# Reordering the side queue of a fused layer: the third pair's projection goes ahead of the second query's rest, the last pair's runs step by step beside the third query

## The chip, the core and the metric

The kernel is one launch on one NeuronCore of a Trainium2 chip. The metric is device time in microseconds (us). Its engines are named as in the profile: PE (matrix multiply; PEld its weight loads), DVE (vector), ACT (scalar, activations), POOL (GpSimd) and SP, which here only issues DMAs. Each engine runs its own list of instructions in order and waits on semaphores for the others.

## The reference, cut to what matters

One layer over 1024 tokens of width 1024, in two sub-layers. The part that matters here:

```python
p = adaln(x, shift1, scale1) @ w_in
y_rw = rwkv7_scan(...)            # state recurrence, in chunks of 64 tokens
y1 = concatenate([y_conv, y_rw]) @ w_out
x  = layer_norm(ALPHA * x + gate1 * y1, ln1_g, ln1_b)
h2 = adaln(x, shift2, scale2)
q  = (h2 @ peer_wq)               # 8 heads x 256
s1, s2 = q-halves against peer_k1, peer_k2   # 128 scores each
v1,i1 = top_k(s1,16); v2,i2 = top_k(s2,16)
sc,ci = top_k(v1[:,None]+v2[None,:], 16)     # 16 of 16384 experts per head
gates = softmax(sc)
y2 = sum_k gelu(h2 . peer_u[e_k]) * gates_k * peer_v[e_k]
out = layer_norm(ALPHA * x + gate2 * y2, ln2_g, ln2_b)
```

## The kernel before, in words

Tokens are cut in eight tiles of 128, and tiles in four pairs of 256. The program has two parts.

**The dense part** comes last and takes over half of the time. For tiles 0 to 4 it multiplies with all 16384 experts, `h2 @ peer_u.T` (line L1285), times a dense matrix of gates, and then `@ peer_v` (L1319). Tiles 5 to 7 are done beside it by gathering their chosen rows (L1203, L1211, L1218). The dense part needs the gate matrices of tiles 0 to 4 in memory (`gmat<-G_d`, L1260).

**The part before it** has these pieces; the short names are used in the prediction.

- The *scan*: the recurrence, 16 chunks (`for c in range(16)`, `solve` and `pass_state`, L615 to L734; L719 writes the state `SN`). It is a chain: chunk after chunk.
- `front(t0)`, F0 to F3, one per pair: loads the scan's and the convolution's output, multiplies it with `w_out` (L822, 96 matmuls of 512 columns with tiles `ychi`, `yclo`, `wsplit`, accumulated in `mm`), adds the residual (L826), normalises twice (L205 to L223, L840, L841) and stores `x1` and, for gathered tiles, `h2`.
- `query(t0)`, Q0 to Q3, one per pair: transposes the normalised rows (L231), multiplies with `wq` (`proj`, L197, 384 matmuls of 256 columns), multiplies with the keys (L894), and, for tiles 0 to 5, finds the best 16 of each 128 scores on DVE (`best16`, L782 to L786 on tiles `vi`, `s12`). Tiles 6 and 7 only store their scores.
- `choose(t)`, C0 to C5: the best 16 of the pairwise sums and their expert numbers, DVE mostly (L930 to L1002). They are put in a queue `slow`.
- `gate_matrix(t)`, G0 to G4: 32 steps a tile. Each step makes a one-hot matrix of four tokens on DVE (`mask`, L1046, one pair per two steps; L1054), POOL (L1053) and ACT (`oa`, L1052), multiplies on PE (L1057, into `mgate`) and copies the result on ACT into `stage` (L1058). Every eight steps a `stage` of 2 MB is written to `G_d` by a DMA from ACT's queue (L1065). There are two `stage` buffers and a third that only every third block of tiles 0 to 3 may use. They are put in a queue `gates`.

F and Q are generators that yield after each matmul or so (F yields twice a matmul). They stand in a list `side`; `step(side)` runs the first of it by one step. During the scan, `fill()` calls `step(side)` between the scan's own matmuls. The list gets F0, Q0 after chunk 3, F1, Q1 after chunk 7 and F2 after chunk 11. Before chunk 9 what is left of the first two (`firsts[:2 + CD]`, CD is 0) is run to its end. After the scan the rest is added and run:

```python
side += [front(S - PB, page2[0]), query(S - 2 * PB), query(S - PB)]   # F3, Q2, Q3
while side or slow or gates:
    step(side)
    fills[0] += 1
    if fills[0] % TSLOW == 0 or not side:     # TSLOW = 2
        slow_step(1)
    if fills[0] % TGATE == 0 or not side:     # TGATE = 12
        with tc.high_priority(offset=GPRI) if GPRI else nullcontext():
            step(gates)
```

So a gate step comes once in twelve steps of `side`, or in every turn when `side` is empty. This order is not the last word: a scheduler takes it as the priorities from which it makes each engine's list, and the waits follow from the data. F0 to F2 take their buffers from a pool of 30 pages (`pgp`), F3 and the choosing of tiles 4 and 5 from a second pool of 12 (`pg2`), which exists after the scan.

Of the kernel before, what the change touches and what calls it, by code (L numbers as in the profile page):

```python
# [21 lines left out]
S = 1024  # L22
# [18 lines left out]
PB = 256  # L41
# [5 lines left out]
GBUF = 6  # L47
AHEAD = 4
NMM = 3

PSG, PSD = 3, 3
SLOW = 4
# [10 lines left out]
CD = 0  # L63
# [23 lines left out]
def layer_kernel(ctx, tc, x, cols, c_row, cond_w, w_in, w2a2, g2, w_out, ln_rows, wq, keys, peer_u, peer_ut, peer_v, peer_vt, out):  # L87
# [47 lines left out]
    fex = ctx.enter_context(ExitStack())  # L135
    psum = fex.enter_context(tc.tile_pool(name="psum", bufs=NMM, space=PSUM))
    ws = fex.enter_context(tc.tile_pool(name="ws", bufs=2))
# [20 lines left out]
    def mm(w=512):  # L158
        return psum.tile([128, 512], F32, tag="mm", name="mm")[:, :w]
# [4 lines left out]
    def page(name, dt=F32, w=512):  # L164
        return pgp.tile([128, max(w, 512)], dt, tag="pg", name=name)[:, :w]
# [6 lines left out]
    def load_split(src, j, scale=None):  # L172

        both = ws.tile([128, 2, KD, 128], F32R, name="wsplit", bufs=WSPLIT)
        hi, lo = both[:, 0], both[:, 1]
        key = src.tensor.name, j
        if key in split_d:
            fetched[key] = ld(both.bitcast(F32), split_d[key])
        else:
            raw = load_raw(src[j])  # L180
            if scale is not None:
                r_ = raw.rearrange("p (k a) b -> p k (a b)", k=2)
                V.tensor_mul(r_, r_, scale[:, None, :].to_broadcast([128, 2, 512]))
            A.activation(hi, raw, AF.Copy)  # L184
            G.tensor_sub(lo, raw, hi.bitcast(F32))  # L185
            split_d[key] = dram.tile([128, 2, KD, 128], F32, name=f"split_{key[0]}{j}")
            ld(split_d[key], both.bitcast(F32))
        return hi, lo

    def proj(w, act, pt):  # L190

        whi, wlo = w
        ahi, alo = act
        i = 0
        for k in range(KD):
            for l, r in ((whi, ahi), (whi, alo), (wlo, ahi)):
                T.matmul(pt, l[:, k, :], r[k], start=i == 0, stop=i == 3 * KD - 1)  # L197
                i += 1
                yield
# [25 lines left out]
    def to_channels(xn, shift, scale, hi, lo, keep=None, ks=range(KD), bank=None):  # L225

        n = 128 * len(xn)
        for k in ks:
            pt = (bank or mm)()[:, :n]
            for i, parts in enumerate(xn):  # L230
                T.transpose(pt[:, 128 * i:128 * i + 128], parts[k // 4][:, 128 * (k % 4):128 * (k % 4) + 128], ident)  # L231
            hf = page("hf", w=n)
            A.activation(hf, pt, AF.Identity, bias=shift(k), scale=scale(k))
            A.activation(hi[k], hf, AF.Copy)
            V.tensor_sub(lo[k], hf, hi[k].bitcast(F32))
            if keep:
                keep(k, hi[k], lo[k])

    def step(jobs):
        while jobs:  # L240
            try:
                next(jobs[0])
                return
            except StopIteration:
                jobs.pop(0)

    def run(jobs):
        for j in jobs:
            yield from j
# [271 lines left out]
    def slow_step(n):  # L521
        for _ in range(n):
            while slow:
                try:
                    next(slow[0])
                    break
                except StopIteration:
                    slow.pop(0)
# [10 lines left out]

    bank = [psr.tile([128, 512], F32, name=f"bank{i}", bufs=1) for i in range(7 - NMM)]  # L540
    turn = [0, 0, 0]
# [6 lines left out]
    def mE(s):  # L548
        return bank[3 + s % (4 - NMM)].rearrange("p (a b) -> p a b", a=4)

# [37 lines left out]
    side, rate, credit, fills = [], [0.0], [0.0], [0]  # L588
# [21 lines left out]
    kept, ys, late, normed, page2, st3, blocks = {}, {}, [], {}, [], [], [0]  # L610
# [164 lines left out]
    def duo(name, dt=F32, pg_=page):  # L775

        ps = [pg_(name, dt).rearrange("p (a t) -> p a t", a=2) for _ in range(KD // 2)]
        return ps, [ps[k // 2][:, k % 2, :] for k in range(KD)]

    def best16(vs, ix, sm):  # L780

        V.max(vs[:, 0:8], sm)  # L782
        V.max_index(ix[:, 0:8], vs[:, 0:8], sm)
        V.match_replace(sm, vs[:, 0:8], sm, -3.0e38)
        V.max(vs[:, 8:16], sm)
        V.max_index(ix[:, 8:16], vs[:, 8:16], sm)  # L786
# [72 lines left out]
    def query(t0):  # L859

        n, nt, tile0 = PB, PB // 128, t0 // 128
        fetch = [tile0 + t in GT for t in range(nt)]
        xn = normed.pop(t0)
        hi, lo = duo("h2hi", F32R)[1], duo("h2lo", F32R)[1]

        def keep(k, h, l):
            for w, f in enumerate((h, l)):
                for t in range(nt):
                    if not fetch[t]:
                        d = 128 * DT.index(tile0 + t)  # L870
                        ld(h2t_d[w, k, :, d:d + 128], f[:, 128 * t:128 * t + 128].bitcast(F32))

        to_channels(xn, lambda k: mod[:, 24 + k:25 + k], lambda k: modp[:, k, 1:2], hi, lo, keep)
        yield
        vi = [page("vi").rearrange("p (q h a r) -> p q h a r", q=2, h=NH, a=2) for t in range(nt)
              if tile0 + t not in score_d]
        val = [t[:, 0] for t in vi]
        idx = [t[:, 1].bitcast(U32) for t in vi]
        for g in range(4):
            kt = pgp.tile([128, 4, 128], F32, tag="pg", name="keys")  # L880
            ld(kt, keys[:, 4 * g:4 * g + 4, :])
            qt = []
            for m in range(4):
                w = load_split(wq, 4 * g + m)
                pt = mm(n)
                yield from proj(w, (hi, lo), pt)
                if m % 2 == 0:
                    qp = page("qt").rearrange("p (a t) -> p a t", a=2)
                A.activation(qp[:, m % 2, :], pt, AF.Copy)
                qt.append(qp[:, m % 2, :])  # L890
            for t in range(nt):
                ps = mm()
                for m in range(4):
                    T.matmul(ps[:, 128 * m:128 * m + 128], qt[m][:, 128 * t:128 * t + 128], kt[:, m, :],  # L894
                             start=True, stop=True)
                s = page("s12")
                A.activation(s, ps, AF.Copy)
                if tile0 + t in score_d:
                    ld(score_d[tile0 + t][g], s)
                    yield  # L900
                    continue
                for m in range(4):
                    best16(val[t][:, 2 * g + m // 2, m % 2], idx[t][:, 2 * g + m // 2, m % 2], s[:, 128 * m:128 * m + 128])
                    yield
        for t in range(len(vi)):
            slow.append(choose(tile0 + t, val[t], idx[t], 0, NH, 4, lambda nm, d, w, p=page2[0] if t0 == S - 2 * PB and P2C else page: p(nm, d, w), V if t0 >= LV else G))
# [166 lines left out]
    flight, firsts = [[solve(1)]], []  # L1073
    for c in range(16):
        if c == 5:
            while side and side[0] is first:
                step(side)
        if c == 9:
            while conv_left and slow:
                slow_step(1)  # L1080
            while side and side[0] in firsts[:2 + CD]:
                step(side)
            fet.close()
            gb.append(fex.enter_context(tc.tile_pool(name="gb", bufs=1)))
        if c < 14:
            flight.append([solve(c + 2)])
        for _ in pass_state(c):
            for i, f in enumerate(flight):
                for _ in range(STEPS[i]):
                    step(f)  # L1090
            step(late)
        if flight:
            f = flight.pop(0)
            while f:
                step(f)
        if c % 4 == 3 and c < 15:
            while late:
                step(late)
            side.append(front(64 * (c - 3), page))
            firsts.append(side[-1])  # L1100
            if c == 3 and CD:
                side.append(run(held))
                firsts.append(side[-1])
            if c < 11:
                side.append(query(64 * (c - 3)))
                firsts.append(side[-1])
            rate[0] = RATES[1]
# [11 lines left out]
    pg2 = pg2x.enter_context(tc.tile_pool(name="pg2", bufs=NP2, side="right"))  # L1119
    page2.append(lambda name, dt=F32, w=512: pg2.tile([128, max(w, 512)], dt, tag="pg2", name=name)[:, :w])  # L1120

    side += [front(S - PB, page2[0]), query(S - 2 * PB), query(S - PB)]
    while side or slow or gates:
        step(side)
        fills[0] += 1
# [263 lines left out]
```

## Time and profile before

| | us |
|---|---|
| median of 3 runs | 3229.51 (3221.18 to 3232.97) |
| the profiled execution | 3222.35, span 3220.4 |
| PE busy in the span | 2995.8 (93%) |
| DVE busy | 2536.9 (79%) |
| POOL busy | 1759.9 (55%) |
| ACT busy | 1168.8 (36%) |
| chain that ended last | PE 41%, DVE 10%, DMA 3% |

The page gives busy time by engine, the span in 40 slices, the chain of work that ended last, and groups of instructions by line. A busy PE is not PE at its peak: matmuls overlap, and the clock that was granted (PEclk) is told beside it. `L12` is line 12 of the kernel before; an order of the kernel after has lines one higher in this part of the program (L823 is L822), and nine higher behind the change.

### The profile page before, as it was taken

Reading aid. Unit: us, or ns where it says so; the run is one execution under the profiler, and the core shown is the slowest. Engines: PE = TensorE matmul, PEld = TensorE weight load, DVE = VectorE, ACT = ScalarE, POOL = GpSimd, SP = SyncE. Lnnn points to the kernel's source line nnn. Section 1 sums busy time; section 2 is a strip of 40 time slices with the busy share of each in tenths; the row PEclk is TensorE's granted clock in tenths of the full one; section 3 lists DMA queues with packets and bytes.
Section 4 is the critical chain, followed back from the end, with each engine's and each line's share of the span. In section 5 each row is a group of like instructions: output and inputs, shape, how many; then the busy total and the mean of one; then the engine's idle time right before and its main releaser. Section 6 shows DMA issues by size and latency. Waiting matters only on the chain.

```text
span 3220.4 us, 53775 instructions
## 1 busy us (share of the span) xinstructions
PE 2995.8 (93%) x19952; PEld 2583.7 (80%) x19952; DVE 2536.9 (79%) x5677; ACT 1168.8 (36%) x2151; POOL 1759.9 (55%) x1368
## 2 busy tenths in 40 slices
PE   6969999899799689899999999899999999999995
PEld 4735676478688579899898888889999898999994
DVE  6379566867977969748999999988778777778788
ACT  5562454253443556543232232322323232222222
POOL 2410112243542543367777776777778777777872
PEclk9979999989799899999999999999999999999998
DMA  8876465378467899989999899899999999999994
GB/s 308 293 208 230 152 177 159 105 260 294 147 195 244 296 303 284 315 312 331 341 328 326 318 317 334 292 332 348 331 347 331 350 330 354 325 349 329 345 332 182
DMA packets 411783, 922.32 MB, mean 286 GB/s; under 512 B 81744, under 2 KB 221568, under 8 KB 389504
## 3 DMA queue, kind: packets, MB, share of 16 engines
q1 hardware_dynamic: 218688, 474.23, 42.8%
q0 software_dynamic: 110592, 402.70, 34.1%
q10 hardware_dynamic: 82240, 41.94, 4.7%
q8 instruction: 157, 2.57, 0.3%
q14 instruction: 106, 0.87, 0.1%
HBM read 788.91 MB, written 129.85 MB: 285 GB/s over the span
## 4 chain that ended last, share of the span: by engine, by line
PE 41%; DVE 10%; DMA 3%; issue 2%; POOL 1%; ACT 0%; ACTq 0%; DVEq 0%; POOLq 0%
PE mg L1285 20%; PE md L1319 20%; DVE grow L1211 2%; DVE gy L1218 2%; DVE yacc L1324 1%; DMA vraw<-peer_vt 1%; DMA grow<-peer_v,eid 1%; DMA grow<-peer_u,eid 1%; POOL vlo L1246 0%; POOL grow L1203 0%; DVE mg L1289 0%; DVE al L1291 0%; PE md L1285 0%; PE mgate L1057 0%; DVE ltkg L983 0%
## 5 line engine op out<-in xcount | busy, mean ns | idle before, releaser
L1285 PE MATMUL mg<-h2h,uhi 128*128 128x320 f32 x2024 | 627.4, 310 | 14.3 <-DVE al L1291 14.3
L1285 PE MATMUL mg<-h2h,ulo 128*128 128x320 f32 x2024 | 626.5, 310 | 0.0
L1285 PE MATMUL mg<-h2l,uhi 128*128 128x320 f32 x2024 | 626.3, 309 | 0.0
L1218 DVE SCALAR_TENSOR_TENSOR gy<-grow,gz,gy 128x1024 f32<-128x1024 f32 x381 | 488.1, 1281 | 15.3 <-DMA grow<-peer_v,eid 13.3
L1319 PE MATMUL md<-vhi,al 128*128 128x512 f32 x1280 | 498.7, 390 | 0.0
L1319 PE MATMUL md<-vhi,ah 128*128 128x512 f32 x1280 | 492.9, 391 | 5.9 <-ACT ah L1290 5.0
L1319 PE MATMUL md<-vlo,ah 128*128 128x512 f32 x1280 | 496.8, 390 | 0.0
L1211 DVE SCALAR_TENSOR_TENSOR grow<-grow,gh 128x1024 f32<-128x1024 f32 x384 | 460.8, 1211 | 22.0 <-DMA grow<-peer_u,eid 21.7
L1203 POOL DMA_INDIRECT grow<-peer_u,eid x384 | 362.3, 944 | 195.0 <-DVE grow L1211 84.0
L1203 POOL DMA_INDIRECT grow<-peer_v,eid x384 | 361.8, 942 | 188.4 <-DVE gy L1218 98.2
L1285 PEld LDWEIGHTS mg<-h2h,uhi 128*128 128x128 f32 x2024 | 381.3, 188 | 22.2 <-DVE al L1291 17.5
L1285 PEld LDWEIGHTS mg<-h2l,uhi 128*128 128x128 f32 x2024 | 381.1, 188 | 4.8
L1285 PEld LDWEIGHTS mg<-h2h,ulo 128*128 128x128 f32 x2024 | 381.1, 188 | 3.0
L1246 POOL TENSOR_TENSOR vlo<-vraw,vhi 128x1024 fp32r<-128x1024 f32 x128 | 309.2, 2415 | 31.1 <-ACT vhi L1244 28.9
L1246 POOL TENSOR_TENSOR ulo<-uraw,uhi 128x1024 fp32r<-128x1024 f32 x128 | 309.3, 2417 | 28.7 <-ACT uhi L1244 26.9
L1324 DVE TENSOR_TENSOR yacc<-md,yacc 128x512 f32<-128x512 f32 x310 | 211.2, 686 | 124.1 <-PE md L1319 123.3
L1053 POOL TENSOR_TENSOR ob<-mask,selt 128x384 f32<-128x384 bf16 x160 | 142.5, 902 | 269.2 <-PE mgate L1057 101.0
L1319 PEld LDWEIGHTS md<-vhi,ah 128*128 128x128 f32 x1280 | 239.9, 188 | 54.2 <-ACT ah L1290 6.5
L1319 PEld LDWEIGHTS md<-vlo,ah 128*128 128x128 f32 x1280 | 240.3, 188 | 49.0
L1244 ACT ACTIVATE vhi<-vraw 128x1024 fp32r<-128x1024 f32 x128 | 135.2, 1056 | 397.8 <-DMA vraw<-peer_vt 397.6
L1319 PEld LDWEIGHTS md<-vhi,al 128*128 128x128 f32 x1280 | 240.3, 188 | 45.3 <-DVE al L1291 0.2
L185 POOL TENSOR_TENSOR wsplit<-wraw,wsplit 128x1024 fp32r<-128x1024 f32 x46 | 115.7, 2518 | 230.5 <-ACT wsplit L184 208.0
(405 smaller groups left out, 5792.4 us busy)
## 6 DMA issues: line engine op xcount, KB each, us to landing
uraw<-peer_ut SPq DMA_DIRECT2D x128, 512.0 KB, 6.8
vraw<-peer_vt SPq DMA_DIRECT2D x128, 512.0 KB, 5.9
wsplit<-split_wq SPq DMA_DIRECT2D x48, 1024.0 KB, 7.5
G_d<-stage ACTq DMA_DIRECT2D x20, 2048.0 KB, 15.7
gmat<-G_d SPq DMA_DIRECT2D x32, 1024.0 KB, 8.0
cw<-cond_w SPq DMA_DIRECT2D x48, 512.0 KB, 5.3
wsplit<-split_w_out SPq DMA_DIRECT2D x24, 1024.0 KB, 6.6
split_w_in<-wsplit SPq DMA_DIRECT2D x22, 1024.0 KB, 5.0
```

What stands on the lines that cost most here:

```text
L185: G.tensor_sub(lo, raw, hi.bitcast(F32))
L1053: G.tensor_mul(ob[:, :3], mb[:, :3], gt[:, c:c + 3, None].to_broadcast([128, 3, 128]))
L1203: G.indirect_dma_start(out=r, out_offset=None, in_=peer_u if k < 128 else peer_v, in_offset=bass.IndirectOffsetOnAxis(ap=eid[:, k % 128:k ...
L1211: V.scalar_tensor_tensor(r, r, 1.0, ht, op0=OP.mult, op1=OP.mult, accum_out=z[:, i:i + 1])
L1218: V.scalar_tensor_tensor(y, r, z[:, i - 128:i - 127], y, op0=OP.mult, op1=OP.add)
L1244: A.activation(hi, raw, AF.Copy)
L1246: G.tensor_sub(lo, raw, hi.bitcast(F32))
L1285: T.matmul(p, l[:, k, :], r[k][:, bs], start=i == 0, stop=i == 3 * KD - 1)
L1319: T.matmul(p, l[:, ts], r[:, e % 2, :], start=e == 0 and q == 0, stop=e == 3 and q == 2)
L1324: ins = V.tensor_add(ya, p, ya)
```

## The change

F2 is put at the head of `side` (for `c` in `AHEADF`, which is chunk 11) and so runs before what is left of Q1. After the scan F3 and Q2 are no longer run one after the other: `beside` does one step of each in a turn. The condition before chunk 9 is written so that it also holds if the head of `side` is another job; at that place the list has the same members as before. The work itself, its tiles and its buffers are the same.

```diff
+AHEADF = 11,
...
-            while side and side[0] in firsts[:2 + CD]:
+            while any(f in side for f in firsts[:2 + CD]):
                 step(side)
...
-            side.append(front(64 * (c - 3), page))
-            firsts.append(side[-1])
+            firsts.append(front(64 * (c - 3), page))
+            side.insert(0 if c in AHEADF else len(side), firsts[-1])
...
-    side += [front(S - PB, page2[0]), query(S - 2 * PB), query(S - PB)]
+    def beside(a, b):
+
+        a, b = [a], [b]
+        while a or b:
+            step(a)
+            step(b)
+            yield
+
+    side += [beside(front(S - PB, page2[0]), query(S - 2 * PB)), query(S - PB)]
```

In numbers of the built programs: Q1 has 266 of its PE instructions behind the scan's last (before: none), F2 one of its 96 (before: all 96), and Q1's searches have 148 DVE instructions behind the scan's last state (before: 40). Between Q3's last PE instruction and G4's last matmul stand 112 of G4's 128 matmuls (before: 20), and 48 dense matmuls in both.

On PE, in the scan of chunk 12 (L663, L705, L689 and their followers L664, L706, L690 are the scan's; L1057 and L1058 are G0's; each row is a line, an operation and out<-in). Before, Q1's projection fills it:

```order
L1057 MATMUL mgate<-oa,ob 128x128 x4
L663 MATMUL bank_1449<-M,AT 64x32 x8
L197 MATMUL mm<-h2hi,wsplit 128x256 x2
L197 MATMUL mm<-h2lo,wsplit 128x256
L197 MATMUL mm<-h2hi,wsplit 128x256 x2
L197 MATMUL mm<-h2lo,wsplit 128x256
L197 MATMUL mm<-h2hi,wsplit 128x256 x2
L705 MATMUL bank_1450<-SN,arl 64x64 x8
```

And after:

```order
L1058 MATMUL mgate<-oa,ob 128x128 x4
L706 MATMUL bank_1450<-SN,arl 64x64 x4
L690 MATMUL bank_1449<-T_8237,MT 64x32 x5
L823 MATMUL mm<-wsplit,yclo 128x512
L823 MATMUL mm<-wsplit,ychi 128x512
L690 MATMUL bank_1449<-T_8237,MT 64x32 x3
L823 MATMUL mm<-wsplit,yclo 128x512
L823 MATMUL mm<-wsplit,ychi 128x512 x2
```

F2's matmuls stand where Q1's stood, and Q1's come later.

On PE, behind the scan, where F3 begins. Before, F3 stands alone with G1:

```order
L822 MATMUL mm<-wsplit,ychi 128x512
L1057 MATMUL mgate<-oa,ob 128x128 x12
L822 MATMUL mm<-wsplit,ychi 128x512
L822 MATMUL mm<-wsplit,yclo 128x512
L822 MATMUL mm<-wsplit,ychi 128x512 x2
```

And after:

```order
L823 MATMUL mm<-wsplit,ychi 128x512
L1058 MATMUL mgate<-oa,ob 128x128 x3
L198 MATMUL mm<-h2hi,wsplit 128x256
L198 MATMUL mm<-h2lo,wsplit 128x256
L198 MATMUL mm<-h2hi,wsplit 128x256 x2
L1058 MATMUL mgate<-oa,ob 128x128 x5
L198 MATMUL mm<-h2lo,wsplit 128x256
L198 MATMUL mm<-h2hi,wsplit 128x256
L823 MATMUL mm<-wsplit,ychi 128x512
```

Q2's projection now stands between the matmuls of F3 and G1.

On PE, at the start of the dense part (L1285 is its first matmul, into `md`, then `mg`; `h2h`, `h2l`, `uhi` and `ulo` are its operands, and Q3 is over). Before, the last two pieces of G4:

```order
L1057 MATMUL mgate<-oa,ob 128x128 x8
L1285 MATMUL md<-h2h_13952,ulo 128x320
L1285 MATMUL md<-h2h_13953,uhi 128x320
L1285 MATMUL md<-h2l_13961,uhi 128x320
L1285 MATMUL md<-h2h_13953,ulo 128x320
L1057 MATMUL mgate<-oa,ob 128x128 x12
L1285 MATMUL mg<-h2h_13946,uhi 128x320
```

And after (L1058 and L1294 are the same lines):

```order
L1058 MATMUL mgate<-oa,ob 128x128 x8
L1294 MATMUL md<-h2h_13951,uhi 128x320
L1294 MATMUL md<-h2l_13959,uhi 128x320
L1294 MATMUL md<-h2h_13951,ulo 128x320
L1294 MATMUL md<-h2h_13952,uhi 128x320
L1294 MATMUL md<-h2l_13960,uhi 128x320
L1294 MATMUL md<-h2h_13952,ulo 128x320
L1294 MATMUL md<-h2h_13953,uhi 128x320
L1294 MATMUL md<-h2l_13961,uhi 128x320
L1294 MATMUL md<-h2h_13953,ulo 128x320
L1058 MATMUL mgate<-oa,ob 128x128 x88
L1294 MATMUL mg<-h2h_13946,uhi 128x320
```

Of the last gate matrix, 88 matmuls, 22 steps, now stand in one piece behind the dense matmuls that could be done ahead of it.

## The prediction, as it was put on record

> **What bounds the kernel now.** I read the slices of the page first, then busy time by stage, then what PE and DVE wait for in the stage that the change rearranges. In the slices, PE is full almost everywhere:
>
> ```profile
> PE   6969999899799689899999999899999999999995
> DVE  6379566867977969748999999988778777778788
> PEclk9979999989799899999999999999999999999998
> DMA  8876465378467899989999899899999999999994
> ```
>
> A slice is 80.5 us. From slice 18 on (1449 us) it is the dense part, which the change doesn't touch. The change works between 880 and 1390 us. By stage (columns: the stretch, its length, then busy us and instruction counts of PE, PEld, DVE, ACT and POOL, then granted clock, DMA share and GB/s):
>
> ```profile
> 880.00:1014.00 134.00, 131.31 (x1586) 118.11 (x1584) 96.07 (x337) 57.23 (x126) 44.97 (x46) 0.99 0.65 209
> 1014.00:1057.00 43.00, 37.14 (x215) 29.78 (x212) 40.87 (x194) 18.95 (x37) 16.15 (x13) 0.92 0.81 284
> 1057.00:1144.00 87.00, 60.58 (x314) 50.65 (x313) 75.80 (x225) 45.68 (x85) 39.22 (x36) 0.80 0.86 277
> 1144.00:1253.00 109.00, 97.29 (x790) 95.40 (x791) 88.25 (x362) 63.48 (x126) 48.19 (x53) 0.97 0.97 316
> 1253.00:1311.00 58.00, 50.73 (x415) 48.40 (x413) 57.48 (x265) 36.59 (x78) 16.74 (x19) 1.00 0.84 269
> 1311.00:1376.00 65.00, 54.29 (x445) 53.29 (x446) 40.52 (x97) 34.06 (x69) 26.02 (x30) 0.95 0.94 316
> 1376.00:1411.00 35.00, 34.78 (x240) 34.24 (x241) 7.72 (x17) 19.82 (x36) 14.80 (x8) 1.00 0.74 246
> ```
>
> The first row is the end of the scan, with Q1 as its filling: PE is full. The second and third are F2 and F3 with G1, C2 and C3: PE idles 32 of 130 us and DVE hardly (13 us). The fourth is Q2, the fifth and sixth Q3, and then the dense part starts. What PE waits for in rows 2 and 3, and then in rows 4 to 6:
>
> ```profile
> PE mgate L1057 <- POOL ob L1053: 18.8, 9, 6.4
> PE mgate L1057 <- DVE ob L1054: 6.9, 4, 4.1
> ...
> PE mgate L1057 <- ACT oa L1052: 14.4, 8, 8.2
> PE mm L197 <- DMA wsplit<-split_wq: 6.9, 4, 3.2
> ```
>
> In rows 2 and 3 it is the gate step, whose POOL and DVE parts come late because DVE is busy with choosing and norms. So the stage alternates: first DVE binds and PE has too little else to do, then both are near full. The marks of the stage are the scan's last state on DVE, the last keys' matmuls of Q3 on PE, and the write of G4's last block:
>
> ```profile
> 1011.74 0.42 DVE L719 TENSOR_TENSOR SN<-SN,bank 128x256 f32<-128x256 f32 x1 [3.74 <-PE bank L716]
> ...
> 1372.95 1.95 PE L894 MATMUL mm<-keys,qt 128*128 128x128 f32 x16
> ...
> 1389.38 0.37 ACTq L1065 DMA_DIRECT2D G_d<-stage  x1
> ```
>
> In both orders 48 dense matmuls stand ahead of G4's last, and the same work behind it. So I take the dense part as shifted by as much as G4's end shifts, and forecast that end (1389 us).
>
> **The change part by part.** Durations:
>
> ```profile
> L783 DVE FIND_INDEX8 vi<-vi,s 128x8 uint32<-128x128 f32 x40 | 10.9, 284 | 0.0
> L784 DVE MATCH_VALUE_LOAD s<-vi,s 128x8 f32 x40 | 3.1, 77 | 0.0
> L205 DVE BATCH_NORM_STATS2 bnst<-xt 128x6 f32<-128x512 f32 x16 | 10.7, 678 | 0.0
> L212 DVE TENSOR_TENSOR rnew<-rstd 128x1 f32<-128x1 f32 x8 | 4.0, 513 | 0.0
> L840 DVE TENSOR_TENSOR xt<-xt,row_g 128x512 f32<-128x512 f32 x8 | 8.6, 1104 | 0.6 <-ACT xt L223 0.6
> L826 DVE SCALAR_TENSOR_TENSOR xt<-xt,mm 128x512 f32<-128x512 f32 x8 | 5.3, 676 | 0.0
> L854 DVE SCALAR_TENSOR_TENSOR xt<-row_sc,xn 128x512 f32<-128x512 f32 x6 | 5.7, 971 | 4.6 <-DMA x_d<-xt 4.0 <-ACT xn L223 0.6
> L1046 DVE TENSOR_TENSOR mask<-iota_b,selbank 128x1024 bf16<-128x1024 bf16 x126 | 84.6, 678 | 7.0 <-POOL ob L1053 3.3 <-ACT oa L1052 1.4 <-ACT selt L1026 1.2
> L1054 DVE TENSOR_TENSOR ob<-mask,selbank 128x128 f32<-128x128 bf16 x127 | 33.4, 279 | 41.8 <-PE mgate L1057 39.9
> L1052 ACT ACTIVATE oa<-mask 128x512 f32<-128x512 bf16 x128 | 79.8, 626 | 14.6 <-PE mgate L1057 5.6 <-issue 3.7 <-DVE mask L1046 3.7
> L1058 ACT ACTIVATE stage<-mgate 128x512 f32<-128x512 f32 x128 | 75.4, 593 | 87.0 <-PE mgate L1057 77.9 <-DMA x_d<-xt 8.8
> ...
> 1368.46 2.04 PE mm L197 x17
> 1128.79 1.05 PE L822 MATMUL mm<-wsplit,ychi 128*128 128x512 f32 x2
> 1135.77 0.63 PE L822 MATMUL mm<-wsplit,ychi 128*128 128x512 f32 x2
> ```
>
> *1. The scan's end.* F2's 96 matmuls take the place of 266 of Q1's. Q1's follow each other at 2.04/17 = 0.12 us: 32 us leave. The spacing of F2's is the row's 0.63 less about 0.40 for one: 0.23 us on a full PE, 22 us come in. The bounds are 10 us earlier (PE is 98% busy there) and 9 us later, if F2's norms hold up the DVE steps of the scan's chain. DVE itself gets lighter: 108 search instructions leave, each 0.28 and for three in five a load of 0.08, 32 us; F2's share comes in: half of the stage's two fronts' norms (5.4 of statistics, about 6 of small ones such as L212), 4.3 of L840, 2.7 of L826 and 1.9 of L854 (two of six), 20 us. I take 7 us earlier: 1005, near the PE bound, since PE has no gap in that stage and the chain's DVE steps wait for PE (3.74 us in the row of the mark).
>
> *2. From there to Q3's end.* DVE was busy 40.87+75.80+88.25+57.48 = 262 of the 297 us from 1014 to 1311, 88%, and to G4's end about 306. Now 32 us of searches are added and 20 of F2 are gone: 318. G4's last 28 steps, 28 x (0.68 + 0.28) = 27 us, fall behind Q3: 291 remain. At 88% that takes 330 us, to 1335; at the 95% of row 2 306 us, to 1311. PE as a check: 300 us busy from 1014 to 1376, plus 34 for Q1, minus about 41 for F2 (at the doubled spacing, 0.43 us, of the row at 1128), minus 27 for G4's 92 moved matmuls: 266 us, at the 83% of 1014 to 1376 again 320 us, 1325; at the 89% of row 4, 1304. I take 1325, between the DVE bounds and nearer the slow one: searches wait for nothing, but the gate steps still do. Before it was 1375. So 50 us are won here: PE fills its idle 32 us, and 27 us of G4 are only put off.
>
> *3. The tail.* Behind Q3 28 gate steps instead of 5. ACT needs 0.63 + 0.59 = 1.22 us for each, 34 us, the lower bound. The upper one comes from the buffers: a block of eight steps takes 10 us, its write lands as this row says, and G4 has two buffers:
>
> ```profile
> G_d<-stage ACTq DMA_DIRECT2D x11, 2048.0 KB, 17.6
> 1358.27 0.38 ACT L889 ACTIVATE qt<-mm 128x256 f32<-128x256 f32 x1 [9.03 <-DMA h2l<-h2t_d]
> ```
>
> Two blocks then take 28 us and four 56; and ACT, which issues the writes, stood 9 us in one such issue. I take 43, with dense loads still light: G4 ends at 1325 + 43 = 1368, 21 us earlier. Before, the tail was 14 us, so the tail gives back 29 of the 50.
>
> *4. Costed at nothing:* the new condition before chunk 9 (same members), `beside` itself (no instruction). F2's loads (8 MB of `w_out`, rows, `x`) go on SP past Q1's weight loads into a stage with a DMA share of 0.65: room, and the pages of F2 and Q1 together only rotate. If that cover fails, step 1's later bound holds. Gate steps come half as often while F3 and Q2 share turns; that is what the tail pays.
>
> The sum against the profiled execution: 3222 - 21 = 3201. It stands 7 us below the median, 3229.5; I forecast the median: 3209.
>
> [...]
>
> **The rivals.**
>
> *Slower: the gate tail.* Gate steps are rationed by turns, and turns became fewer. If blocks follow their writes strictly (56 us) and another issue blocks ACT for 9 us, the tail is 65. With Q3's end at 1340 G4 ends at 1405: 16 us later, 3246. It decides from a tail over 64 us at 1325, or 54 at 1335. For it: the 9 us row, and the writes' 17.6 us. Against: a third of the buffers' wait lies under work that was already there before.
>
> *Same: DVE stays the bound.* Q3's end at 1335, tail 48: 1383, 6 us, 3223. Or the scan ends 9 us later: likewise. For it: rows 2 and 5. PE's idle time then only moves.
>
> *Much faster: the clock.* Row 3 has a granted clock of 0.80, and F3's matmuls come at 0.43 us there against 0.23 later. If PE is kept fed, F3's half at the slow spacing saves some 10 us and the gate matmuls likewise: Q3's end at 1305, tail 40, G4's end at 1345, 44 us: 3186. [...] Against a large gain: DVE, not PE, sets the pace there.
>
> **How the numbers follow.** Sum as forecast (13 to 35 us won): 0.48. Clock: 0.08. Same: 0.28. Slower: 0.16. The bound of what a measurement tells is 0.5%, 16 us. A part of the first case lies within it: faster 0.48, same 0.36, slower 0.16. The range takes in the bounds: early 1311 + 34 = 1345, 44 us, 3186; late 1335 + 56 + 5 = 1396 and some 5 us of spread among the runs, 3242. The likeliest case's own is 3194 to 3217.
>
> **What the profile after would show.** The scan's last state at 1002 to 1012. PE over 85% busy from there to Q3's end, where it was 60.58 of 87; the clock in that stretch near 0.95. The waits of `mgate` for `ob` (18.8 and 6.9) halved. Q3's last keys' matmul at 1311 to 1340, the last write of `G_d` at 1355 to 1385, with waits of PE for ACT's `oa` or of ACT for writes between the two. The dense part as long as before, to 5 us. I am wrong if Q3's end moves by less than 30 us, if the tail takes over 55, or if the scan gets longer.

## The result, and the profile after

The changed kernel takes 3203.87 us (median of 5 runs, 3197.76 to 3213.42) against 3226.74 (5 runs) for the kernel before on the same chip: ratio 0.9941, 95% interval 0.9926 to 0.9956. By the ratio that is faster by 0.6%, some 19 us (the two medians lie 22.9 us apart); forecast were 3209 and a range from 3186 to 3242. The profiled execution took 3205.98 us, its span is 3204.2.

The slices of the page after (same engines and order as before):

```profile
PE   6969999899799888899999999999999999999995
DVE  6379566867957899548999999988778777778788
PEclk9979998989789999999999999999999999999998
DMA  8876465378477998989999989899999989999994
```

The slice at 1046 us, the 14th, had 6 tenths of PE and 9 of DVE; now it has 8 and 8. By stretches (same columns as before: the stretch, its length, then busy us and counts of PE, PEld, DVE, ACT, POOL, granted clock, DMA share, GB/s). First the kernel before, from the scan's end to G4's end, then three stretches of the kernel after:

```profile
1014.00:1389.00 375.00, 312.80 (x2268) 290.10 (x2265) 303.48 (x1142) 206.78 (x407) 148.48 (x153) 0.93 0.89 294
```

```profile
880.00:1014.00 134.00, 126.03 (x1355) 104.67 (x1355) 89.56 (x223) 56.22 (x118) 57.75 (x55) 0.90 0.68 220
1057.00:1144.00 87.00, 67.82 (x447) 61.89 (x446) 74.22 (x354) 39.41 (x83) 25.74 (x28) 0.90 0.91 298
...
1014.00:1376.00 362.00, 317.29 (x2477) 301.82 (x2475) 299.28 (x1251) 200.91 (x408) 135.07 (x143) 0.97 0.90 300
```

PE's idle time between the scan's end and G4's end went from 375 - 312.80 = 62 us to 362 - 317.29 = 45. The stretch of 87 us in which F3 had stood alone has 67.82 us of PE for 60.58, and a clock of 0.90 for 0.80. The marks that the prediction used, in the timeline of the kernel after, are the scan's state on DVE, Q3's last keys on PE, and the issue of G4's last write on ACT:

```profile
1009.72 0.40 DVE L720 TENSOR_TENSOR SN<-SN,bank 128x256 f32<-128x256 f32 x1
...
1331.77 0.61 PE L895 MATMUL mm<-keys,qt 128*128 128x128 f32 x4
...
1375.46 0.37 ACTq L1066 DMA_DIRECT2D G_d<-stage  x1
```

Q3 ends 43 us earlier than before, G4 only 14. What PE waits for from 1014 to 1376 us, longest first:

```profile
PE mgate L1058 <- POOL ob L1054: 13.2, 16, 1.6
PE mgate L1058 <- ACT oa L1053: 11.1, 8, 5.0
PE mm L895 <- ACT qt L890: 6.4, 1, 6.4
PE mm L823 <- ACT s L898: 4.8, 1, 4.8
```

The long waits of the gate step for `ob` are gone: the longest is 1.6 us where it was 6.4. So far the profile looks as forecast. What sets G4's end is told by two other views. The first is the chain of work that ended last, around G4's end. Before, it ran over Q3's matmuls and the dense ones on PE:

```profile
1368.46 2.04 PE mm L197 x17
1370.50 0.89 PE mgate L1057 x8
1371.39 0.48 PE mm L197 x4
...
1373.12 1.57 PE mm L894 x14
...
1375.85 6.72 PE md L1285 x44
1382.57 1.35 PE mgate L1057 x12
```

After, it runs over DVE's searches and masks from 1243 to 1280, and then over the writes of the gate blocks, their `stage` buffers and the load of what was written:

```profile
1282.65 18.77 DMA G_d<-stage
1301.50 14.32 DMA G_d<-stage
...
1319.83 7.14 DMA h2h<-h2t_d
1327.05 0.37 ACTq L1066
...
1340.71 15.39 DMA G_d<-stage
...
1366.44 10.28 DMA G_d<-stage
1376.78 5.86 DMA gmat<-G_d
```

The second view is PE's gate matmuls alone, G2, G3 and G4, each with a stretch that holds it, up to 5 us wider than from its first matmul to its last (256 matmul records are its 32 steps; the busy figure is PE's). Before, and then after:

```profile
1146.00:1226.00 80.00, 35.53 (x256) 0.96 0.94 310
1232.00:1306.00 74.00, 34.45 (x256) 1.00 0.88 283
1314.00:1389.00 75.00, 34.25 (x256) 0.95 0.89 307
```

```profile
1152.00:1232.00 80.00, 34.31 (x256) 1.00 0.92 308
1241.00:1317.00 76.00, 33.75 (x255) 1.00 0.88 298
1319.00:1376.00 57.00, 36.03 (x256) 0.94 0.89 284
```

The gate matrices run one behind another. From first matmul to last they took 75, 73 and 74 us, and now take 78, 76 and 55. Only G4 has become shorter, by 18 us: most of its steps now lie behind Q3, and there a step comes every 1.1 to 1.9 us (blocks of eight are written at 1340.71, 1356.19, 1366.44 and 1375.46), while beside a query it takes 2.3 to 2.4.

The pause between G3 and G4 has shrunk too, from 8.7 us to 2.0. G4 needs, besides G3's end, the choosing of tile 4, whose results PE transposes first. Before, and then after:

```profile
L1023 PE MATMUL selbank<-ident,tkg x3: 272/273/329, 1305.9 to 1307.8; 128*128 128x128 f32 x3
```

```profile
L1024 PE MATMUL selbank<-ident,tkg x3: 272/272/273, 1276.6 to 1277.1; 128*128 128x128 f32 x3
```

Before, these stood right at G3's end (1305.6), and PE sat idle for DVE's last results ahead of them, so tile 4's choosing held G4 back as much as G3 did. After, they are 40 us ahead of G3's end (1317.4), as Q2, from which tile 4 is chosen, runs earlier. On the other side, G2 starts 6 us later than before, and why is in SP's and PE's timelines. G2 needs the choosing of tile 2, which goes through memory (`sel_d`). Before, it was there long before G1 was through, and the loads went out right behind G1's last steps:

```profile
1132.16 1.89 SPq L1017 DMA_DIRECT2D ob<-sel_d  x3
...
1142.02 0.49 PE L1023 MATMUL selbank<-ident,ob 128*128 128x128 f32 x3
1146.54 1.95 PE L1057 MATMUL mgate<-oa,ob 128*128 128x128 f32 x16
```

After, G1 is through earlier (its last matmuls are the row at 1119.14), but Q1's searches now lie behind the scan, and tile 2 is chosen only at 1127:

```profile
1127.12 0.32 SPq L968 DMA_DIRECT2D sel_d<-tkg  x1
1128.26 7.83 SPq L968 DMA_DIRECT2D sel_d<-tkg  x2
1136.18 0.38 SPq L1018 DMA_DIRECT2D ob<-sel_d  x1
1138.72 0.32 SPq L1018 DMA_DIRECT2D ob<-sel_d  x1
...
1119.14 1.05 PE L1058 MATMUL mgate<-oa,ob 128*128 128x128 f32 x8
1152.48 1.95 PE L1058 MATMUL mgate<-oa,ob 128*128 128x128 f32 x16
```

32 us pass without a gate step (12 before). Not all of that is the choosing. Tile 2's last write went out at 1128.26; the second issue in that row, at 1135.77, is tile 3's first write. It waited 7.4 us for DVE, and two of tile 2's three loads stood behind it in SP's list. PE had transposed what they brought by 1142.3, and DVE made G2's first masks only at 1147.5, behind other work. So there are two theories of what the change won: filling PE's idle time (the prediction's), or a chain of gate matrices whose start the change delays and whose last link it quickens. The experiments tell them apart.

### The profile page after: what moved, and what is told of

It is laid out like the page before. It is cut to its first block, busy times and chain, and to the rows that moved or that the text cites. A ratio compares the mean times of both kernels' runs of the same rounds, so it can differ in the third digit from the quotient of the medians.

```text
span 3204.2 us, 53805 instructions
## 1 busy us (share of the span) xinstructions
PE 2993.7 (93%) x19952; PEld 2579.7 (81%) x19952; DVE 2513.0 (78%) x5677; ACT 1162.4 (36%) x2148; POOL 1761.6 (55%) x1368
## 4 chain that ended last, share of the span: by engine, by line
PE 39%; DVE 12%; DMA 5%; issue 3%; POOL 1%; ACT 1%; SPq 0%; POOLq 0%; ACTq 0%; DVEq 0%
PE mg L1294 20%; PE md L1328 19%; DVE grow L1220 2%; DMA G_d<-stage 2%; DVE gy L1227 2%; DVE yacc L1333 1%; DMA grow<-peer_v,eid 1%; DMA vraw<-peer_vt 1%; POOL grow L1212 1%; DMA grow<-peer_u,eid 1%; POOL ulo L1255 1%; DVE mg L1298 0%; DVE ltkg L984 0%; DVE al L1300 0%; PE mgate L1058 0%
## 5 line engine op out<-in xcount | busy, mean ns | idle before, releaser
L1294 PE MATMUL mg<-h2h,uhi 128*128 128x320 f32 x2024 | 627.9, 310 | 12.6 <-DVE al L1300 9.5
L1294 PE MATMUL mg<-h2l,uhi 128*128 128x320 f32 x2024 | 626.3, 309 | 0.0
L1294 PE MATMUL mg<-h2h,ulo 128*128 128x320 f32 x2024 | 626.2, 310 | 0.0
L1220 DVE SCALAR_TENSOR_TENSOR grow<-grow,gh 128x1024 f32<-128x1024 f32 x384 | 460.9, 1212 | 39.0 <-DMA grow<-peer_u,eid 35.7
L1294 PEld LDWEIGHTS mg<-h2h,uhi 128*128 128x128 f32 x2024 | 381.3, 188 | 21.7 <-DVE al L1300 13.3
L1294 PEld LDWEIGHTS mg<-h2l,uhi 128*128 128x128 f32 x2024 | 381.3, 188 | 4.8
L1294 PEld LDWEIGHTS mg<-h2h,ulo 128*128 128x128 f32 x2024 | 381.1, 188 | 2.8
```

Source lines behind the costliest of these rows:

```text
L1220: V.scalar_tensor_tensor(r, r, 1.0, ht, op0=OP.mult, op1=OP.mult, accum_out=z[:, i:i + 1])
L1294: T.matmul(p, l[:, k, :], r[k][:, bs], start=i == 0, stop=i == 3 * KD - 1)
```

## The experiments

All are compared by ratio with the kernel before, run on the same chip. Runs e8 to e10 are one execution each and have no ratio. The table has the marks of each profiled execution in us, counted from the first busy instruction (0.3 us less than in the rows above): the scan's last state operation, G2's first matmul, Q3's last, G4's last, and three lengths: the stage (scan's end to G4's end), the dense part (to its last matmul) and what lies behind it.

| kernel | scan | G2 | Q3 | G4 | stage | dense | behind | ratio (95%) |
|---|---|---|---|---|---|---|---|---|
| before | 1011.9 | 1146.3 | 1374.7 | 1388.0 | 376.0 | 1795.2 | 37.0 | 1 |
| e8, before again | 1010.4 | 1147.5 | 1377.3 | 1390.6 | 380.2 | 1798.6 | 37.1 | |
| after | 1011.9 | 1152.2 | 1332.1 | 1374.5 | 362.6 | 1794.9 | 34.5 | 0.9941 (0.9926 to 0.9956) |
| e10, after again | 1010.2 | 1153.3 | 1334.7 | 1375.5 | 365.3 | 1792.3 | 34.6 | |
| e1, front only | 1011.6 | 1156.8 | 1359.4 | 1382.7 | 371.1 | 1789.4 | 34.5 | 0.9967 (0.9955 to 0.998) |
| e2, beside only | 1006.4 | 1125.5 | 1387.1 | 1397.3 | 390.8 | 1787.0 | 36.9 | 0.9987 (0.9976 to 0.9999) |
| e3, less DVE | 1012.0 | 1140.8 | 1316.0 | 1367.8 | 355.9 | 1790.1 | 34.5 | 0.9933 (0.9915 to 0.9951) |
| e4, F3 twice, after | 1014.5 | 1139.7 | 1360.3 | 1378.7 | 364.2 | 1798.2 | 35.7 | 0.998 (0.9966 to 0.9994) |
| e5, F3 twice, before | 1003.8 | 1144.1 | 1366.5 | 1381.0 | 377.2 | 1781.9 | 35.7 | 0.9938 (0.9922 to 0.9954) |
| e9, e5 again | 1005.0 | 1144.3 | 1369.1 | 1383.6 | 378.6 | 1784.8 | 35.7 | |
| e6, gates twice as often | 1012.7 | 1152.6 | 1335.2 | 1377.2 | 364.5 | 1789.6 | 34.5 | 0.9919 (0.9901 to 0.9937) |
| e7, front beside the rest | 1005.7 | 1189.8 | 1372.1 | 1408.2 | 402.5 | 1785.9 | 34.6 | 1.0038 (1.0026 to 1.0051) |
| e11, half of G3 | 1012.2 | 1154.1 | 1343.2 | 1354.1 | 341.9 | 1795.6 | 35.2 | 0.9907 (0.9889 to 0.9926) |
| e12, choosing on POOL | 1013.0 | 1181.3 | 1325.3 | 1394.6 | 381.6 | 1792.4 | 34.5 | 0.9993 (0.9981 to 1.0006) |

### The two halves of the change (e1, e2)

F2 goes in front, but F3 and Q2 run one after the other:

```diff
-    side += [beside(front(S - PB, page2[0]), query(S - 2 * PB)), query(S - PB)]
+    side += [front(S - PB, page2[0]), query(S - 2 * PB), query(S - PB)]
```

> The change without `beside`: F2 goes ahead of Q1's rest, but F3, Q2 and Q3 run one after the other. Theory (interleaving: PE's idle 32 us behind the scan are filled because something else stands beside the stage in which DVE binds): only half of it is left, since F3 stands alone with G1 again while DVE chooses for tiles 2 and 3; about 3215. Rival A (F2's place in the scan is the whole gain): 3204, like the full change. Rival B (`beside` is the whole gain): 3226, like before.

F3 and Q2 share turns, but F2 stays behind the scan:

```diff
-AHEADF = 11,
+AHEADF = ()
```

> The change without F2's move: Q1 fills the scan as before, F2 stands alone behind it, then F3 and Q2 run step by step. Theory (interleaving): Q2 fills PE while DVE chooses for tiles 2 and 3, and the choosing starts as early as before, but F2 still stands alone; about 3214. Rival A (F2's place is the whole gain): 3226. Rival B (`beside` is the whole gain): 3204.

Measured: 3211.08 us, 0.9967, and 3219.46 us, 0.9987. F2 in front alone gives over half of the ratio, the turns alone 0.1%. The stage says it more sharply: with F2 in front it is 7 us shorter than the mean of the two executions before (378.1), with the turns alone 13 us longer (390.8), and with both 14 us shorter (364.0). The two are not additive: `beside` pays only when F2 is through. Without that Q2 ends late, tile 4 is chosen late (its transposes on PE start at 1319 us, in the changed kernel at 1277), and the gate steps stop between 1289 us and G4's start at 1325. That e2 is still no slower than before lies outside the stage: scan and dense part together were 15 us shorter. This asked for the next runs, since neither half of the change touches the dense part.

### Is PE the bound of the stage? (e4, e5)

Each of F3's 96 matmuls is done twice, in the changed kernel and then in the kernel before (the line of the first matmul, of which only the mark of the last one changes, is left out):

```diff
...
+                            if t0 == S - PB:
+                                T.matmul(acc[t], l[k][:, ts], r, start=False, stop=k == KD - 1 and q == 2)
```

> The changed kernel with each of F3's 96 matmuls done twice into the same sum: 96 x 0.23 = 22 us more on PE between 1083 and 1162, nothing more on any other engine. If PE is the bound of the changed stage: 15 to 22 us later, 3219 to 3226. If DVE is: 5 us at most, 3204 to 3209.

> The kernel before with each of F3's 96 matmuls done twice (its sums are then twice as large; nothing else changes). It is the other half of the run in which the same 96 extra matmuls cost the changed kernel 12.6 us. Theory (in the old order PE had room exactly there: 26 us idle in the 87 us in which F3 ran, behind DVE; the change wins by filling that room): the extra matmuls, 22 us at the quick spacing of 0.23 us, go mostly into idle time, and the kernel is at most 6 us slower than before, ratio 1.000 to 1.002. Rival (PE is the bound of the stage in the old order as well, and the change won by something else, the clock or the transfers): 12 to 22 us slower, ratio 1.004 to 1.007. A third: the extra matmuls raise the granted clock of 0.80 there, and the kernel is no slower or even faster, ratio 0.998 to 1.000.

Measured: 3215.45 us, 0.998, and 3205.64 us, 0.9938. By the ratios alone the first would say that PE binds the changed kernel (12.6 us of 22), and the second would be absurd: more work, and faster than any of the three expectations allowed. The stage tells more. PE was busy 16 to 17 us longer in it in both kernels, and it lasted 364.2 us for 364.0 and 377.2 for 378.1. For the kernel before that is clean: Q3's end, counted from the scan's end, did not move either (means of 363.4 us for 364.9, with the runs of the next section), and G2, counted so, started 2 to 6 us later, not earlier. There the extra work went into idle time, and PE's work does not set G4's end. For the changed kernel e4 does not show it. Q3's end, counted from the scan's end, came 23 us later (345.8 for a mean of 322.4), as much as all of the extra work, and the stage kept its length while G2 began 12 us earlier, which may have hidden a cost. The stretch of e5 in which F3 lies shows where it went, 8 us more of PE and a higher clock than the 0.80 before:

```profile
1057.00:1144.00 87.00, 68.54 (x351) 58.72 (x352) 64.63 (x207) 38.86 (x70) 34.46 (x35) 0.88 0.78 252
```

### Where e5's 21 us come from (e8, e9, e10)

The same three kernels once more, with a profile.

> The kernel before once more, unchanged, for a second profiled execution. The first stood at 1011.9 us at the scan's last state, 376.0 from there to G4's end, 1795.2 from there to the last dense matmul, 37.0 behind it. The kernel with F3's matmuls doubled stood at 1003.8, 377.2, 1781.9 and 35.7: its 22 us less lie in the scan and the dense part, which the edit does not touch. Theory (these two lengths scatter from one execution to another): the scan's end differs by 4 us or more from 1011.9, or the dense part by 6 or more from 1795. Rival (they belong to the build, whose order on the engines differs in the dense part): scan's end within 2 us of 1011.9 and the dense part within 3 us of 1795.

> The kernel before with F3's matmuls done twice, once more, for a second profiled execution (its sums are twice as large there). Scatter: the scan's end moves from 1003.8 toward 1008 to 1012, the dense part from 1781.9 to 1785 or more. Rival (build): 1002 to 1006 and 1779 to 1785. In both the stage between is within 5 us of 377, if the 22 us of extra matmuls really lie in idle time there.

> The changed kernel once more, unchanged, for a second profiled execution. The first stood at 1011.9 us at the scan's last state, 362.6 from there to G4's end, 1794.9 for the dense part, 34.5 behind it. If the stage between the scan and G4's end is what the change won, 13.4 us, it stays within 4 us of 362.6, while scan and dense part may scatter by 5 and 8 us. Rival (the stage scatters as much as the others): 368 us or more.

They repeat (table): scan's ends within 2 us, stages within 4.2, dense parts within 3.4, and the two kernels stay apart by 7 and 14 us in scan and dense part. As far as two executions of each can tell, scatter is out: these lengths belong to the build. In the dense part the orders differ, and PE stands idle less in it, here from 1411 to 2211 us, before and then e5:

```profile
1411.00:2211.00 800.00, 779.83 (x4344) 707.58 (x4343) 727.47 (x1519) 236.53 (x392) 593.61 (x455) 1.00 0.91 327
```

```profile
1411.00:2211.00 800.00, 789.91 (x4411) 716.10 (x4410) 714.38 (x1533) 241.31 (x395) 606.82 (x463) 1.00 0.92 334
```

In the scan, though, all five engines have the same instructions in the same order in both builds up to 1043 us of the kernel before, where SP's lists part first, and the two still part by 3.4 us between 660 and 760 (1.6 in the second pair), with different granted clocks (shown at the end). What in the build does that stays open. For the change itself the sum is now clean, with the mean of two executions each: scan -0.1, stage -14.1, dense part -3.3, behind it -2.5, together -20.0 us against 19 by the ratio. Since a build moved parts that its edit leaves alone by 7 and 14 us, a difference of 7 or 8 us in the stage, as in e1 and e3, is weak evidence. The larger ones, each at a named link of the row, carry the argument.

### Is DVE the bound? (e3)

In Q1's part, the best 8 are found once and copied, so the second searches of tiles 2 and 3 are left out:

```diff
...
+                    if t0 == PB:
+                        V.max(vs_[:, 0:8], sm_)
+                        V.max_index(ix_[:, 0:8], vs_[:, 0:8], sm_)
+                        V.tensor_copy(vs_[:, 8:16], vs_[:, 0:8])
+                        V.tensor_copy(ix_[:, 8:16], ix_[:, 0:8])
+                    else:
+                        best16(vs_, ix_, sm_)
```

> The changed kernel; of Q1's 32 searches the second half (the next eight) is left out and the first eight are copied instead, so some 0.7 us less of DVE for each, 22 us in all, between the scan's end and the choosing for tiles 2 and 3. If DVE is the bound there (my DVE sum, 291 us to Q3's end): the end of the gate matrices comes 12 to 22 us earlier, 3182 to 3192. If PE is the bound now: 5 us at most, 3199 to 3204.

Measured: 3199.95 us, 0.9933, an interval that covers the changed kernel's ratio. DVE was busy 15 us less in the stage. Q3's end came 16 us earlier, G4's end 7: G2 started 11 us earlier (1140.8 for 1152.2, tile 2 was chosen earlier), and the three gate matrices took 5 us longer. So Q3's end follows DVE (and, by e4, PE as well), but G4's end does not follow Q3's.

### Is it the rationing of gate steps? (e6)

```diff
-TGATE = 12
+TGATE = 6
```

> The changed kernel with TGATE 6 for 12: a gate step is queued once in six turns of the side list. It tests the reason that the prediction gave for the tail behind the third query (gate steps come half as often while two jobs share a turn). Theory of the prediction: with twice as many, G4's steps no longer stand behind Q3, the tail shrinks from 43 to some 20 us while Q3's end comes at most 10 us later, and the kernel is 8 to 13 us faster than the changed one: ratio to the kernel before 0.990 to 0.992. Rival (the tail comes from the data: the gate matrices run one behind another, and G2 starts only when the choosing of tile 2 is done, 1127 us now and 1074 before): the tail stays at 38 to 48 us and the ratio within 0.993 to 0.996.

Measured: 3200.21 us, 0.9919; the interval overlaps the changed kernel's. The tail stayed at 42 us and the stage at 364.5. PE's order had hardly changed: G4's first matmul comes 3 us behind G3's last, so what keeps G4's steps behind Q3 is G3 in front of them, not the number of turns. The reason that the prediction gave for the tail falls.

### Filling PE's last gaps (e7)

```diff
+    def chain(*js):
+        for j in js:
+            yield from j
-    side += [beside(front(S - PB, page2[0]), query(S - 2 * PB)), query(S - PB)]
+    side[:] = [beside(front(S - PB, page2[0]), chain(*side, query(S - 2 * PB))), query(S - PB)]
```

> The changed kernel, but F3 goes beside what is left of Q1 and then Q2, in place of beside Q2 alone. The longest waits of PE left in the changed kernel between the scan and the tail stand where one job runs alone: 6.4 us for Q1's last keys (nothing else is queued there), 4.8 us for the scores' copy. Theory (PE's idle time, 53 us between 880 us and G4's end where it was 65, is what sets the end, so filling it wins): these 11 us come back, and the kernel is 6 to 12 us faster than the changed one, ratio to the kernel before 0.990 to 0.992. Rival: F3 needs the last chunk's rows, which are in memory only some us behind the scan, so its matmuls stand in front of Q1's and hold PE up for 5 to 15 us: ratio 0.994 to 0.999. Another: it only moves the waits, 0.9935 to 0.995.

Measured: 3235.04 us, 1.0038, slower than both. It was to win 6 to 12 us by PE's gaps and lost 38 us in the stage. Neither rival had the reason right: F3 slowed Q1's rest, tile 2 was chosen 55 us later (1182 for 1127), and G2 could not start. Its loads on SP, its first matmuls and G4's last write:

```profile
1183.62 0.80 SPq L1018 DMA_DIRECT2D ob<-sel_d  x2
...
1190.03 2.08 PE L1058 MATMUL mgate<-oa,ob 128*128 128x128 f32 x8 [3.33 <-POOL ob L1054]
...
1409.16 0.42 ACTq L1066 DMA_DIRECT2D G_d<-stage  x1
```

### The chain of gate matrices by itself (e11, e12)

Half of G3's steps are left out, which shortens one link of the chain:

```diff
+                if tt == DT[3] and q >= TB // 2:
+                    A.activation(stage[:, :, q:q + 4], pt.rearrange("p t e -> p e t"), AF.Copy)
+                    yield
+                    continue
```

> The changed kernel, but G3 makes only the first four of every eight steps; for the other four ACT copies the last result again, and their masks, operands and matmuls are left out (16 of G3's 32 steps, so the output differs). Work left out: 64 gate matmuls and about 16 x (0.68 + 0.28) = 15 us of DVE. The stage between the scan's last state and G4's end is 364 us in the changed kernel; 96 extra matmuls of 17 us in it moved it by nothing, 16 us less of DVE shortened it by 8. Theory (the gate matrices run one behind another and each takes 55 to 80 us for its 32 steps whatever PE and DVE do beside it; their chain sets G4's end): G3 takes some 40 us for 76 and the stage becomes 325 to 340 us. Rival (the sum of DVE's work sets it, at the half price that the run with less DVE showed): 354 to 360 us. A third (PE's work): 358 us or more.

Reductions of the choosing of tiles 2 and 3 go from DVE to POOL, which takes work off DVE and makes the start of the chain later:

```diff
-LV = 256
+LV = 512
```

> The changed kernel with LV 512 for 256: 40 reductions of the choosing of tiles 2 and 3 go from DVE to POOL, 17 us of DVE by their rows (8 of 0.68, 24 of some 0.38, 8 of 0.28), 41 us on POOL, which is busy 135 us of the 363. Theory (DVE holds the stage up in part, as 16 us less of it shortened the stage by 8): the stage is 5 to 9 us shorter than 364, and the ratio to the kernel before is 0.9915 to 0.993. Rival (the reductions lie on the path to G2, and POOL needs more than twice as long for each): C2 is done later than 1127 us, G2 starts later, and the stage is 5 to 15 us longer, ratio 0.996 to 0.999.

Measured: e11 3188.87 us, 0.9907, stage 341.9, which is 22 us shorter. That is just outside the chain's 325 to 340, and far from the 354 to 360 of DVE's work. G3 did halve, from 76 to 39 us, and Q3's end came 11 us later; G4 then ran more beside Q3 and took 68 us for 55, so the next link took back 13 of the 36 us. G3's 16 steps still took 2.5 us each though its four blocks were all written, so the writes do not set its pace; what does was not tested. e12 3219.95 us, 0.9993, stage 381.6, 18 us longer: the rival, by more than its 5 to 15 us. It is the plainest of all, since DVE was busy 7 us less and Q3 ended 7 us earlier than in the changed kernel, and G4 ended 20 us later, because G2 began 29 us later. (PE's waits for POOL's `ob` in the gate steps stayed at 13 us, so POOL's extra work did not hold the steps themselves.) The loads for G2 on SP, G2's first matmuls, Q3's last, and G4's last write:

```profile
1162.90 0.32 SPq L1018 DMA_DIRECT2D ob<-sel_d  x1
...
1181.59 1.95 PE L1058 MATMUL mgate<-oa,ob 128*128 128x128 f32 x16
...
1324.91 0.61 PE L895 MATMUL mm<-keys,qt 128*128 128x128 f32 x4
...
1395.49 0.37 ACTq L1066 DMA_DIRECT2D G_d<-stage  x1
```

No kernel that computes the same beat the changed one, except that e6's lead of 0.2% is not told apart. What the runs point to, tile 2 chosen by the time G1 ends (1120 us), was not tried: Q1's searches would have to go ahead of F2's norms on DVE.

## Why the prediction was right, and where not

**Step 1, the scan's end, 1005, at most 10 us earlier or 9 later than before: held by its bounds, but the gain hardly came.** By the prediction's mark it is 1009.72 for 1011.74, by the operation behind it the same within 0.1. PE did get lighter in the scan (126.03 us for 131.31, and DVE 89.56 for 96.07), and the end did not follow. Why stays open: e5's build moved the same mark by 7 us without an edit there. (The searches that leave DVE add up, by the step's own terms, to 35 us and not to 32; that changes no bound.)

**Step 2, Q3's end, 1325: 1332, inside the bounds of 1311 to 1335.** The sum of DVE's work at 88% had given 1335, and e3 shows that Q3's end does follow DVE; e4 shows that it follows PE too. That "PE fills its idle 32 us" was half right. From 1057 to 1144 it filled 7 of 26 us, and 17 of 62 in the whole stage.

**Step 3, the tail, 43 us: 43.** The size was right, and both bounds lay about it (ACT's 34 us and the writes' 56): ACT did stand 9 us, though not for the issue itself (see the last section), and writes of `stage` are on the chain. Its meaning was wrong. The prediction took the tail as the price that "gives back 29 of the 50". By the runs it is where the time is won: G4's 32 steps took 55 us, most of them there, and 74 beside Q3, while G2 and G3 each got 3 us longer. The reason given, that gate steps "come half as often", fell with e6.

**The sum, 21 us for G4's end: 14.** It was Q3's end (7 us off) plus the tail (exact), so as arithmetic only step 2 was mis-sized. But Q3's end was the wrong thing to start from. Over the runs it lies between 1316 and 1387 us, and the order of G4's ends is another: 1325 goes with 1395 in e12, and 1360 with 1379 in e4. The row of jobs that ends there is G2's start and three gate matrices: 1146 + 242 before, 1152 + 222 after, 1190 + 218 in e7, 1181 + 213 in e12. Neither term is fixed. A later start leaves more of G4 behind Q3, where it is quicker, and in e2 the row stood 36 us for tile 4 (1126 + 272). From before to after, G4's end moved 6 us later by G2's start and 6 by G2, G3 and the pause between them, and 7 earlier by the pause before G4 and 18 by G4. So Q3's end does matter, but only by the steps of G4 that are left behind it, and Q2's by the choosing of tile 4.

**Step 4, costed at nothing: mostly.** F2's loads cost nothing that shows; PE waits 0.8 us for `split_w_out` in the stage. Not costed at all was that F2 in front of Q1's rest puts off Q1's searches, and with them tile 2 and G2. It cost 32 us without a gate step for 12 before, of which 6 show in G2's start, since G1 became quicker (81 us for 92).

**The dense part as long as before, to 5 us:** right by the first executions (1794.9 for 1795.2) and by the means (-3.3). The 2.5 us behind it came on top. With 14 in the stage they make the 20; the forecast had all 21 in the stage. That the total came out so near is luck in part: 6 of the 20 us came from parts that the prediction expected to stay as they were.

**The rivals.** The slower one, a tail over 64 us, did not come, but its neighbour exists: e7 is slower by a late start of the same gates. The same-time rival had G4's end at 1383 through DVE; it was nearer to G4's end than the clock rival (1345), and its place, DVE, is real for Q3's end, and for G4's only as far as it puts off a choosing. The clock rose as the third rival said (0.90 for 0.80), and that it won little is argued, not shown: e5 raised it to 0.88 with F3's matmuls doubled, and the stage kept its length. That a PE kept fed is granted a higher clock was the author's estimate, and no run shows it as a rule: in the 87 us of F3's old stretch 60.58, 67.82 and 68.54 us of PE went with 0.80, 0.90 and 0.88, but from 660 to 760 us 96.42 went with 0.85 and 94.26 with 0.91. Of the signs that were named, PE's 85% from the scan's end to Q3's end, the halved waits for `ob`, Q3's end and the last write came. The clock near 0.95 in F3's old stretch did not.

Interleaving by itself did not win. Both halves together made the stage 14 us shorter, but interleaving alone (e2) made it 13 us longer and interleaving more (e7) 24, because the choosing that a gate matrix starts from came later, of tile 4 in e2 and of tile 2 in e7.

## What to carry to other kernels

Where jobs hang on one another in a row (here choosing, then gate matrices, then the write and the dense part), predict the start of the row, the pace of each link and every other result that a link waits for, before any sum of busy time: here DVE was busy 83% and PE 88% of the changed stage, and neither's sum gave its end. Ask of each job that is put in front which result it puts off, and who starts with that result. And when one build's order differs from another's, compare lengths stage by stage: of e5's difference of 0.6%, 7 and 14 us came from the scan and the dense part, which its edit does not touch, so doubling work was no clean test by the total alone.

## What the runs showed of the hardware that was not expected

With the same instructions in the same order on all five engines, the kernel before and e5 had different granted clocks from 660 to 760 us, and each nearly the same again in a second execution (0.85 and 0.83; 0.91 and 0.91). Before, and then e5:

```profile
660.00:760.00 100.00, 96.42 (x1116) 85.25 (x1116) 59.78 (x249) 48.16 (x94) 42.22 (x23) 0.85 0.80 273
```

```profile
660.00:760.00 100.00, 94.26 (x1154) 83.81 (x1154) 61.62 (x278) 48.23 (x94) 41.98 (x24) 0.91 0.83 288
```

What looked like a second finding is the program's own. ACT, which had to issue a write of `G_d`, stood, by the profile's releaser, until a load of `h2h` from SP's queue was through, 8.95 us here and 9.03 in the kernel before. The trace's semaphores tell why: the write was given the semaphore (106; 108 before) that signals the landing of that very load (in the kernel before, of a load of `h2l`), and ACT waits for it first: the last of the load's 16 landings is at 1326.98 us (1357.78 before), and ACT goes on at 1327.00 (1357.80). The program's two queues share semaphores, and it has ACT wait until the first use of one is over. The chain after runs through this wait (7.14 us of `h2h<-h2t_d`).

```profile
1327.52 0.63 ACT L1053 ACTIVATE oa<-mask 128x512 f32<-128x512 bf16 x1 [8.95 <-DMA h2h<-h2t_d]
```
